# Split weight tiles begin 64, 256, 400 and 464 bytes behind a multiple of 512, and a scan mask is kept in bf16

## The chip, the cores and the metric

The kernel runs on one core of one Trainium2 chip. The metric is the device time of one execution in microseconds, the median of several runs. A run is also profiled once; its rows are in microseconds from the start of the profiled span unless marked ns.

## The reference

One decoder layer for 1024 tokens of width 1024, in float32. After a norm, one wide projection feeds two mixers: RWKV-7 time mixing (8 heads of 64, a recurrent state for each) and attention over at most 256 keys that an indexer selects for each query. Their outputs are merged through sigmoid gates, and a SwiGLU network with 2816 hidden channels follows.

```python
u = rmsnorm(h, norm1_g)
proj = u @ w_in                       # 1024 x 5960
p_rwkv, p_att, p_idx, p_gate = jnp.split(proj, c, axis=-1)
y_a = rwkv7_mix(token_shift(p_rwkv, tshift_mu), ...)
y_b = dsa_attention(q, k, v, q_idx, k_idx, w_idx)
g_a, g_b = jnp.split(jax.nn.sigmoid(p_gate), 2, axis=-1)
merged = g_a * (y_a @ w_o_rwkv) + g_b * (y_b @ w_o_att)
h = h + merged @ w_out
z = rmsnorm(h, norm2_g) @ w_ffn_in
z_gate, z_up = jnp.split(z, 2, axis=-1)
h = h + (jax.nn.silu(z_gate) * z_up) @ w_ffn_out
return rmsnorm(h, normf_g)
```

## The kernel before

The 1024 tokens are two halves of 512. Every large product has activations with channels on the partitions as the moving operand, 128 channels by 512 tokens at a time, and a 128x128 block of weights as the stationary one; a result tile of 128 output channels by 512 tokens gathers in PSUM over eight blocks of input channels (six in the last group of the SwiGLU network).

To keep float32 accuracy in the faster fp32r format, each operand is split into a high part and the rest: hi = x rounded to fp32r, lo = x - hi. `mm3` (L133 to L144) then issues three matmuls for each block: hi weights by hi activations (L138) and by lo activations (L139), in turn block by block, and afterwards lo weights by hi activations (L143). Each matmul is preceded by a load of its own 128x128 weights.

Weights come tile by tile through `weights` (L122 to L129). A DMA brings 128 partitions x 8 blocks x 128 float32, 4096 bytes a partition, into a tile `wst` (three buffers). `split` (L111) makes `whi` on ScalarE (L112) and `wlo` on VectorE (L113, which reads `wst` and `whi`); each has two buffers. All of these tiles begin at a multiple of 512 bytes in their partition, and so does each 512-byte block in them; activations that stream through the matmuls begin at multiples of 512 as well. 231 weight tiles pass through in one execution.

TensorE's order is written out by hand: the program's generators yield after a few matmuls each, and `pump` lets projections, the merge and the SwiGLU network run as fill between the steps of the indexer, RWKV and attention, which are chains of short matmuls with VectorE and ScalarE between. The other engines' orders come from the scheduler, and the splits of weights have a high priority there. Small temporaries `tmp` come in turn from a ring of four buffers of 128x512 float32.

RWKV works on quarters of 256 tokens. Its decay is a running sum in chunks of 64 tokens: `tensor_tensor_scan` (L535) multiplies the sum by a mask, `rmask`, which is 0 at the first token of a chunk and 1 elsewhere, and adds the next value. There are four scans of 128x256 in each quarter, 16 in all. `rwkv_consts` fetches the mask once (L477, on SyncE's queue) at about 348 us, and the tile is float32, 1024 bytes a partition.

Of the kernel before, what the change touches and what calls it, by code (L numbers as in the profile page):

```python
# [11 lines left out]
F32 = mybir.dt.float32  # L12
F32R = mybir.dt.float32r
BF16 = mybir.dt.bfloat16
# [35 lines left out]
def block_kernel(ctx: ExitStack, tc: tile.TileContext, ins: dict, outT: bass.AP, stop=None, dbg=None):  # L50
    nc = tc.nc
    V, A, G, T, SY = nc.vector, nc.scalar, nc.gpsimd, nc.tensor, nc.sync

    cp = ctx.enter_context(tc.tile_pool(name="cp", bufs=1))
    wp = ctx.enter_context(tc.tile_pool(name="wp", bufs=2))
# [52 lines left out]
    def tmp():  # L108
        return tp.tile([128, HT], F32, tag="tmp", name="tmp")

    def split(hi, lo, x):  # L111
        A.activation(hi, x, AF.Copy)  # L112
        V.tensor_tensor(lo, x, hi.bitcast(F32), op=ALU.subtract)  # L113
# [3 lines left out]
    def raw_weights(src, nk=8):  # L117
        st = wp.tile([128, nk, 128], F32, tag="wst", name="wst", bufs=3)
        wq[0].dma_start(st, src)
        return st  # L120

    def weights(src, nk=8, rush=True, st=None):  # L122
        with tc.high_priority() if rush else nullcontext():
            if st is None:
                st = raw_weights(src, nk)
            hi = wp.tile([128, nk, 128], F32R, tag="whi", name="whi")
            lo = wp.tile([128, nk, 128], F32R, tag="wlo", name="wlo")
            split(hi, lo, st)
        return hi, lo  # L129

# [134 lines left out]
    def proj(ct, us, out, off=0):  # L265
        w = weights(ins["w_in"][ct])
        for half, u in enumerate(us):
            ps = acc()
            o = off if half == 0 else 0
            yield from mm3(ps[:, :HT - o], w, u, tok=slice(o, HT))  # L270
            out(half, ps)
# [45 lines left out]
    def proj_rope(ct, us, pj, cs, dst, scale=1.0, off=0):  # L317

        wa, wb = weights(ins["w_in"][ct]), weights(ins["w_in"][ct + 1])
        for half, u in enumerate(us):  # L320
            o = off if half == 0 else 0
            ps = acc()
            yield from mm3(ps[:, :HT - o], wa, u, tok=slice(o, HT))
            ab = rope_a(cs, ps, half, o, scale)
            ps = acc()
            yield from mm3(ps[:, :HT - o], wb, u, tok=slice(o, HT))
            rope_b(cs, ps, ab, pj, dst(half), half, o, scale)
# [12 lines left out]
    def first(us, xp, pj, cp2, cs):  # L340
# [6 lines left out]
        load_x(1, hs[1], range(8))  # L347
        SY.dma_start(cs, ins["rope"])
        ws = [weights(None, st=st, rush=False) for st in (st0, st1)]
        sqs, raws = [], []  # L350
        for half, h in enumerate(hs):
# [117 lines left out]
    def rwkv_consts(p):  # L469
        blk = p.tile([128, 128], F32, name="blk")  # L470
        SY.dma_start(blk, ins["consts"][:, K_BO, :])
        wup = p.tile([128, 512], F32, name="wup")
        SY.dma_start(wup, ins["wa_up"])
        gup = p.tile([128, 512], F32, name="gup")
        SY.dma_start(gup, ins["g_up"])
        rmask = p.tile([128, 256], F32, name="rmask")
        SY.dma_start(rmask, ins["rmask"])  # L477
        ind8 = p.tile([8, 512], F32R, name="ind8")
        t = tmp()
        SY.dma_start(t[0:8, :], ins["ind8"])  # L480
        A.activation(ind8, t[0:8, :], AF.Copy)
        for tag, n in [("wa", 256), ("gd", 256), ("x0", 1024), ("x7", 1024), ("v", 1024), ("x1", 1024), ("x2", 1024),
                       ("x4", 1024), ("x5", 1024), ("x3", 1024), ("AR", 2048), ("rhs", 512), ("UV0", 1024),
                       ("UV1", 1024), ("BK0", 1024), ("BK1", 1024), ("x6", 1024)]:
            p.tile([128, n], F32, tag=tag, name=tag)
        cmask = p.tile([128, 192], F32, name="cmask")
        SY.dma_start(cmask, ins["cmask"])
        p.tile([128, 64], F32, name="edge")
        ind2 = smp.tile([128, 2], F32, name="ind2")
        SY.dma_start(ind2, ins["ind2"])  # L490

        return blk, cmask, wup, gup, rmask, ind2, ind8
# [764 lines left out]
    wq[0] = A  # L1257
    sr, rp = opened("right", "rw")
    consts = rwkv_consts(rp)
    at0 = []  # L1260

# [127 lines left out]
```

## Time and profile before

| | |
|---|---|
| median of 3 runs | 1791.27 us (1788.14 to 1796.37) |
| the profiled execution | 1791.53 us, span 1789.7 us |
| granted TensorE clock, mean | 0.987 |
| PE matmul busy | 1735.4 us, 97% |
| PE weight load busy | 1428.1 us, 80% |
| VectorE / ScalarE busy | 1113.0 us / 829.6 us |
| HBM traffic | 135 GB/s over the span |

PE is TensorE's matmuls, PEld its weight loads, which overlap them; DVE is VectorE, ACT ScalarE, POOL GpSimd, SP SyncE, and a q behind an engine's name is its queue. A row of a timeline gives the start, the length, the engine, the line in the kernel, the operation and how many like ones in a row were merged; a bracket behind it tells how long the engine had been idle, and what ended that. A row of a tile's answer gives the number of instructions and their shortest, median and longest time in ns. Matmuls are pipelined, so their shown lengths overlap, and the ends of matmuls are modelled.

### The profile page before, as it was taken

The numbers are of one execution on the slowest core, as the hardware profiler recorded it, in microseconds if no ns is written. First come the engines' busy times: TensorE is split into PE (matmuls) and PEld (weight loads), VectorE is DVE, ScalarE is ACT, GpSimd is POOL, SyncE is SP. The second block draws the span as 40 slices with busy tenths as digits, with TensorE's granted clock in tenths as the row PEclk, the third lists the DMA queues.
The fourth block names the chain that finished last, engine by engine and source line by source line (L and its number), as shares of the span: only waits on it lengthen the run. The fifth ranks groups of instructions, "written<-read, shape, count | busy, mean of one in ns | idle before, by whom it ended". The sixth has DMA issues, their size and how long they took to land.

```text
span 1789.7 us, 26478 instructions
## 1 busy us (share of the span) xinstructions
PE 1735.4 (97%) x10112; PEld 1428.1 (80%) x10112; DVE 1113.0 (62%) x2113; ACT 829.6 (46%) x1527; POOL 94.4 (5%) x116
## 2 busy tenths in 40 slices
PE   7999999999999899999999999999999999999997
PEld 6888888788887677777788788888788888888875
DVE  6779899866568358958865455434575564454454
ACT  6355998543455886345333355522334332232232
POOL 0000000010020010001001211000000000000000
PEclk9999999999999899999999999999999999999998
DMA  5542224536275434643243944143555344434432
GB/s 205 164 137 94 97 98 142 169 88 178 90 210 150 119 113 146 215 123 104 78 118 118 261 122 124 60 149 120 183 186 166 114 142 145 138 96 148 143 100 103
DMA packets 129838, 243.97 MB, mean 136 GB/s; under 512 B 36408, under 2 KB 57528, under 8 KB 129584
## 3 DMA queue, kind: packets, MB, share of 16 engines
q1 hardware_dynamic: 106752, 169.95, 30.7%
q10 hardware_dynamic: 15120, 46.18, 8.3%
q0 software_dynamic: 7840, 26.15, 5.4%
q8 instruction: 80, 1.31, 0.3%
q14 instruction: 46, 0.38, 0.1%
HBM read 189.29 MB, written 52.95 MB: 135 GB/s over the span
## 4 chain that ended last, share of the span: by engine, by line
PE 74%; DVE 11%; ACT 6%; issue 5%; DMA 3%; POOL 0%; DVEq 0%; POOLq 0%; ACTq 0%
PE acc L138 20%; PE acc L139 19%; PE acc L143 19%; PE mix L1016 2%; PE mix L992 2%; PE mix L1006 2%; DVE wlo L113 2%; ACT junk L907 2%; ACT junkl L907 2%; PE mix L859 1%; DMA wst<-in_w_ffn_in 1%; DVE junk L904 1%; PE mix L764 1%; PE mix L752 1%; PE mix L638 1%
## 5 line engine op out<-in xcount | busy, mean ns | idle before, releaser
L113 DVE TENSOR_TENSOR wlo<-wst,whi 128x1024 fp32r<-128x1024 f32 (+1 forms) x231 | 278.2, 1204 | 356.9 <-PE acc L143 165.7
L112 ACT ACTIVATE whi<-wst 128x1024 fp32r<-128x1024 f32 (+1 forms) x231 | 241.0, 1044 | 315.7 <-PE acc L139 266.6
L138 PE MATMUL acc<-zhi,whi 128*128 128x512 f32 x672 | 266.7, 397 | 2.0 <-DVE tmp L1164 2.0
L139 PE MATMUL acc<-zlo,whi 128*128 128x512 f32 x672 | 262.8, 391 | 0.0
L143 PE MATMUL acc<-zhi,wlo 128*128 128x512 f32 x672 | 171.6, 393 | 0.0
L138 PEld LDWEIGHTS acc<-zhi,whi 128*128 128x128 f32 x672 | 126.6, 188 | 29.1 <-DVE tmp L1164 2.4
L139 PEld LDWEIGHTS acc<-zlo,whi 128*128 128x128 f32 x672 | 126.8, 189 | 24.6
L143 PEld LDWEIGHTS acc<-zhi,wlo 128*128 128x128 f32 x672 | 124.4, 188 | 25.6 <-issue 1.0
L138 PE MATMUL acc<-u1hi,whi 128*128 128x512 f32 x352 | 141.4, 402 | 0.0
L138 PE MATMUL acc<-fhi,whi 128*128 128x512 f32 x352 | 138.6, 394 | 2.5 <-ACT fhi L112 2.5
L138 PE MATMUL acc<-u0hi,whi 128*128 128x512 f32 (+1 forms) x352 | 135.7, 388 | 4.2 <-DVE tmp L280 2.4
L139 PE MATMUL acc<-flo,whi 128*128 128x512 f32 x352 | 137.8, 392 | 0.9 <-DVE flo L113 0.9
L139 PE MATMUL acc<-u1lo,whi 128*128 128x512 f32 x352 | 138.6, 394 | 0.0
L139 PE MATMUL acc<-u0lo,whi 128*128 128x512 f32 (+1 forms) x352 | 134.1, 383 | 0.0
L143 PE MATMUL acc<-u1hi,wlo 128*128 128x512 f32 x352 | 90.7, 398 | 0.0
L143 PE MATMUL acc<-fhi,wlo 128*128 128x512 f32 x352 | 89.0, 393 | 0.0
L143 PE MATMUL acc<-u0hi,wlo 128*128 128x512 f32 (+1 forms) x352 | 86.8, 387 | 0.0
L112 ACT ACTIVATE fhi<-tmp 128x512 fp32r<-128x512 f32 x44 | 27.8, 631 | 120.0 <-DVE tmp L1168 119.9
L138 PEld LDWEIGHTS acc<-fhi,whi 128*128 128x128 f32 x352 | 66.4, 189 | 18.3 <-ACT fhi L112 4.2
L138 PEld LDWEIGHTS acc<-u0hi,whi 128*128 128x128 f32 x352 | 66.3, 188 | 17.5 <-issue 2.6
L139 PEld LDWEIGHTS acc<-flo,whi 128*128 128x128 f32 x352 | 66.4, 189 | 15.7 <-DVE flo L113 2.2
L138 PEld LDWEIGHTS acc<-u1hi,whi 128*128 128x128 f32 x352 | 66.9, 190 | 14.3 <-issue 0.9
(302 smaller groups left out, 3143.7 us busy)
## 6 DMA issues: line engine op xcount, KB each, us to landing
wst<-in_w_ffn_in SPq DMA_DIRECT2D x72, 512.0 KB, 3.6
wst<-in_w_in ACTq DMA_DIRECT2D x36, 512.0 KB, 3.7
wst<-in_w_fo SPq DMA_DIRECT2D x28, 512.0 KB, 3.6
wst<-in_w_in SPq DMA_DIRECT2D x27, 512.0 KB, 3.6
k<-d_k POOLq DMA_DIRECT2D x24, 512.0 KB, 9.0
h<-in_xT SPq DMA_DIRECT2D x32, 256.0 KB, 5.2
d_g<-tmp ACTq DMA_DIRECT2D x32, 256.0 KB, 3.0
tmp<-d_g SPq DMA_DIRECT2D x32, 256.0 KB, 3.1
```

The lines of the kernel that those rows point to most:

```text
L112: A.activation(hi, x, AF.Copy)
L113: V.tensor_tensor(lo, x, hi.bitcast(F32), op=ALU.subtract)
L138: T.matmul(ps, whi[:, wk + k, :], ahi[:, ak + k, tok], start=k == 0, stop=False)
L139: T.matmul(ps, whi[:, wk + k, :], alo[:, ak + k, tok], start=False, stop=False)
L143: T.matmul(ps, wlo[:, wk + k, :], ahi[:, ak + k, tok], start=False, stop=k == nk - 1)
L638: T.matmul(pss[g][:, hh * 128:(hh + 1) * 128], BK[ct // 2][ro, ct % 2, pr, 2 * pa:2 * pa + 2, :].rearrange("p s t -> p (s t)"), AR[ro, ct, ...
L752: T.matmul(as_[h % 2][:, ct * 64:ct * 64 + 64], AR[ro, ct, c, :, :].rearrange("p s t -> p (s t)"), st[ro, ct, :], start=True, stop=True)
L764: T.matmul(ps[ba:ba + 64, hc], TT[ba:ba + 64, pr, h, :], rhs[ba:ba + 64, hc], start=True, stop=True)
L907: A.activation(junka[:, :n], y, AF.Sign, bias=z[:, i:i + 1], accum_out=cnt[:, i:i + 1])
L992: T.matmul(ps[:, :w], q[bi // 2][:, e, bi % 2 * 128:bi % 2 * 128 + 128], k[:, i, e, c:c + w], start=i == 0, stop=i == 1)
L1006: T.transpose(ps[:, j * 128:(j + 1) * 128], L[:, (c + j) * 128:(c + j + 1) * 128], ident)
L1016: T.matmul(py[64 * e:64 * e + 64, bi * 128:(bi + 1) * 128], v[:, j, 64 * e:64 * e + 64], pts[e][j // 4][:, j % 4, :], start=j == b, stop=j ...
```

## The change

`whi` and `wlo` are allocated as tiles of 1024 + 48 and 1024 + 16 float32 a partition, and the 1024 that are used begin 16 and 4 float32 behind the tile's start. With two buffers of each, one behind the other, the used parts begin 64 and 256 bytes (whi) and 400 and 464 bytes (wlo) behind a multiple of 512. A six-block tile takes the first 768 of the 1024. This needs 512 bytes a partition more.

The mask becomes bf16, which needs 512 bytes less: its values arrive as float32 in a `tmp` tile, and VectorE copies them into the bf16 tile. All other tiles that move do so by exactly 512 bytes. TensorE's instructions and their order are the same as before; VectorE has one more, the copy.

```diff
+    def place(tag, off, more, nk):
+        w = wp.tile([128, 1024 + more], F32R, tag=tag, name=tag)
+        return w[:, off:off + nk * 128].rearrange("p (k c) -> p k c", k=nk)
+
     def weights(src, nk=8, rush=True, st=None):
         with tc.high_priority() if rush else nullcontext():
             if st is None:
                 st = raw_weights(src, nk)
-            hi = wp.tile([128, nk, 128], F32R, tag="whi", name="whi")
-            lo = wp.tile([128, nk, 128], F32R, tag="wlo", name="wlo")
+            hi, lo = place("whi", 16, 48, nk), place("wlo", 4, 16, nk)
             split(hi, lo, st)
         return hi, lo
...
-        rmask = p.tile([128, 256], F32, name="rmask")
-        SY.dma_start(rmask, ins["rmask"])
+        rmask = p.tile([128, 256], BF16, name="rmask")
+        t = tmp()
+        SY.dma_start(t[:, 0:256], ins["rmask"])
+        V.tensor_copy(rmask, t[:, 0:256])
         ind8 = p.tile([8, 512], F32R, name="ind8")
```

## The prediction

> **What bounds the kernel now.** I read the page's busy shares and its chain of waits first, then the rows of the tile wlo, then the timeline at places where matmuls of known width stand in a row.
>
> ```profile
> span 1789.7 us, 26478 instructions
> PE 1735.4 (97%) x10112; PEld 1428.1 (80%) x10112; DVE 1113.0 (62%) x2113; ACT 829.6 (46%) x1527; POOL 94.4 (5%) x116
> PE 74%; DVE 11%; ACT 6%; issue 5%; DMA 3%; POOL 0%; DVEq 0%; POOLq 0%; ACTq 0%
> PE acc L138 20%; PE acc L139 19%; PE acc L143 19%; PE mix L1016 2%; PE mix L992 2%; PE mix L1006 2%; DVE wlo L113 2%; ACT junk L907 2%; ACT junkl L907 2%; PE mix L859 1%; DMA wst<-in_w_ffn_in 1%; DVE junk L904 1%; PE mix L764 1%; PE mix L752 1%; PE mix L638 1%
> ```
>
> TensorE sets the time: 74% of the chain is PE, and 58% are the three lines whose weights come out of the tiles that move: L138 and L139 read whi, L143 reads wlo. So the question is whether a place of these tiles changes the pace of those matmuls. A weight load is a separate instruction on PEld that runs beside the matmul before it.
>
> How many there are comes from the rows of the tile wlo:
>
> ```profile
> L143 PEld LDWEIGHTS acc<-zhi,wlo x672: 186/188/192, 848.1 to 1739.0; 128*128 128x128 f32 x168
> L143 PE MATMUL acc<-zhi,wlo x672: 387/389/504, 848.3 to 1739.2; 128*128 128x512 f32 x168
> L143 PE MATMUL acc<-u0hi,wlo x352: 279/389/504, 45.2 to 510.5; 128*128 128x512 f32 x164, 128*128 128x256 f32 x12
> L143 PE MATMUL acc<-u1hi,wlo x352: 387/389/632, 50.7 to 693.4; 128*128 128x512 f32 x176
> L143 PE MATMUL acc<-fhi,wlo x352: 388/389/628, 953.3 to 1773.5; 128*128 128x512 f32 x176
> L143 PE MATMUL acc<-yhi,wlo x128: 387/389/397, 707.3 to 1337.7; 128*128 128x512 f32 x128
> L143 PE MATMUL acc<-mhi,wlo x128: 387/389/793, 756.3 to 1383.5; 128*128 128x512 f32 x128
> ```
>
> The first row is the loads (188 ns each as shown). The counts of the matmuls, ahead of the colon, make 1984; 12 of the 176 sampled u0 rows are 256 wide, so about 24 of its 352 are. That leaves about 1960 wlo matmuls of 512 columns, and by the code twice as many with whi: 5880 in all.
>
> Their pace, and that of narrower ones (start, length of the merged stretch, count at the end):
>
> ```profile
> 1562.53 1.98 PE L143 MATMUL acc<-zhi,wlo 128*128 128x512 f32 x8
> 35.90 1.12 PE L143 MATMUL mix<-u0hi,wlo 128*128 128x256 f32 x8
> 1419.13 1.05 PE L240 MATMUL mix<-kc,rs 128*128 128x128 f32 x8
> L240 PE MATMUL mix<-kc,rs x32: 271/275/581, 843.7 to 1780.2; 128*128 128x128 f32 x32
> ```
>
> A matmul is shown as 0.389 us long, but they are pipelined; start to start is (1.98 - 0.389) / 7 = 0.2273 us at 512 columns. At 256 columns, whose shortest row is 279 ns, it is (1.12 - 0.28) / 7 = 0.120 us. At 128 columns, each with a load of its own, it is (1.05 - 0.275) / 7 = 0.111 us. So 256 columns more cost 0.1073 us, 512 columns cost 0.2146, and 0.0127 us of each matmul does not scale with its width. And a load of 128 columns together with its short matmul needs no more than 0.111 us, less than half of the 0.227 that the wide matmul beside it gives. 5880 x 0.2273 = 1337 us of the 1790 go at this pace.
>
> **The change part by part.** *The places.* All weight tiles begin at a multiple of 512 bytes now; afterwards the two whi buffers begin 64 and 256 behind one, the two wlo buffers 400 and 464. Number, size, order and buffering of loads, splits and matmuls stay. Three accesses see the new places: PE's weight loads, ACT's write of whi, and DVE's read of whi and write of wlo.
>
> Weight loads first. If they took time from the matmul that streams beside them, a matmul with no load beside it would end earlier. The trace has that case, in the last two output tiles of the kernel:
>
> ```profile
> 1768.25 1.52 PE L143 MATMUL acc<-fhi,wlo 128*128 128x512 f32 x6
> 1769.61 0.39 PE L138 MATMUL acc<-fhi,whi 128*128 128x512 f32 x1
> 1769.81 0.69 DVE L1188 TENSOR_TENSOR h<-h,acc 128x512 f32<-128x512 f32 x1 [1.08 <-PE acc L143]
> 1772.33 1.52 PE L143 MATMUL acc<-fhi,wlo 128*128 128x512 f32 x6
> 1773.89 0.69 DVE L1188 TENSOR_TENSOR h<-h,acc 128x512 f32<-128x512 f32 x1 [2.00 <-PE acc L143]
> 1776.07 0.97 PEld L227 LDWEIGHTS mix<-kc,sacc 128*128 128x128 f32 x8 [2.65 <-DVE sacc L221]
> ```
>
> The ends that the profile gives for matmuls are modelled, so I take the waiting VectorE as the clock. In the first group the sixth matmul starts at 1768.25 + 1.52 - 0.389 = 1769.38, the next matmul (whose weights must be loaded meanwhile) follows at 1769.61, and L1188 starts at 1769.81: 0.43 us after. In the second group the sixth starts at 1773.46, no load comes until 1776.07, and L1188 starts at 1773.89: again 0.43. Rounding to 0.01 us hardly leaves room for 0.0127 us, so at today's places the load takes nothing from the matmul beside it.
>
> Now a load from another place. No row shows a 128-column block that starts off a multiple of 512. From below its price is nothing; from above it may grow from at most 0.111 us to 0.227, about double, before the matmul beside it stops covering it. I take nothing, because the nearest rows, the loads of today, show no meeting with the stream and more than half of the cover unused. [...]
>
> ACT and DVE:
>
> ```profile
> L112 ACT ACTIVATE whi<-wst x231: 831/1061/1067, 4.7 to 1764.4; 128x1024 fp32r<-128x1024 f32 x108, 128x768 fp32r<-128x768 f32 x8
> L113 DVE TENSOR_TENSOR wlo<-wst,whi x231: 951/1224/1227, 7.9 to 1765.8; 128x1024 fp32r<-128x1024 f32 x108, 128x768 fp32r<-128x768 f32 x8
> ACT whi L112 <- PE acc L139: 266.6, 164, 5.3
> ```
>
> One pair of tiles is split in 1.06 + 1.22 = 2.3 us and feeds 24 matmuls of 0.227 = 5.4 us, and ACT stands waiting 266.6 us in all for PE to give a whi buffer back. A few ns more or less on a split are hidden by that wait; were the cover gone, 10 ns on each of 231 pairs would be 2.3 us.
>
> *The mask.* A 128x256 DMA goes into a tmp tile, DVE copies it to bf16, and the 16 scans read the copy. The rows of that time:
>
> ```profile
> 347.26 0.29 DVE L532 TENSOR_SCALAR gd<-gd 128x256 f32<-128x256 f32 x1
> 347.79 0.68 SPq L477 DMA_DIRECT2D rmask<-in_rmask  x1
> 350.28 1.23 DVE L113 TENSOR_TENSOR wlo<-wst,whi 128x1024 fp32r<-128x1024 f32 x1 [2.73 <-ACT whi L112]
> 353.54 2.13 PE L143 MATMUL acc<-u0hi,wlo 128*128 128x512 f32 x8
> 354.43 0.77 DVE L551 TENSOR_SCALAR x<-x,hb 128x256 f32<-128x256 f32 x2 [2.92 <-ACT x L528]
> DMA to landing us min/median/max: 4.2/4.2/4.2
> L535 DVE TENSOR_TENSOR_SCAN x<-rmask,x x16: 662/666/685, 356.4 to 841.5; 128x256 f32<-128x256 f32 x16
> ```
>
> In the order of the changed program the copy stands on DVE right behind L532 and ahead of that wlo split. Issued at 347.79 and landing 4.2 later, the mask is there at 352.0; the copy, priced by L532 on the same 128x256, ends at 352.3. So the split, queued behind the wait, moves from 350.28 to 352.3 and ends at 353.5 instead of 351.5; PE's L143 on it begins at 353.54. The wait of 2 us is just covered: I count 0.1 us for it, and up to 1 if the transfer is later. The next on DVE, L551, waits for ACT until 354.43 anyway. The transfer keeps its place and size in SP's queue. The tile taken from the ring of four tmp tiles shifts which buffer each later tmp gets, not how many there are; around here ACT gets a wait on the copy before it may reuse that buffer, two raw tiles later (356), past the copy's end. The scans: VectorE reads one operand narrower; from 0 to, if a scan were halved, -16 x 0.33 = -5 us, at most partly on the chain; I take 0, as the other operand and the result stay f32 and 666 ns for 256 elements is no matter of bytes.
>
> **Sum.** The profiled execution took 1791.53 us with a span of 1789.7, beside a median of 1791.27 (1788.14 to 1796.37). 1791.53 + 0 + 0 + 0.1 = 1791.6; put on the median, 1791.4. I say 1791.5, with 1788 to 1796 as this case's own range. What a measurement of this kernel can tell from no change is about 0.5%, 9 us, so "same" reaches from 1782 to 1800.
>
> **Rivals.** *Faster:* the fixed 0.0127 us of each matmul comes from operands that all begin at the same place behind a multiple of 512, the streamed ones and the weights, and spreading the places takes it away. For it: that part is there at 512 and at 256 columns alike, as a cost per load would be. Against it: the 0.43 and 0.43 above. If only wlo gains (64 and 256 are still multiples of 64, 400 and 464 are not), 1960 x 0.0127 = 25 us: 1766. If all gain, 5880 x 0.0127 = 75 us: 1717. [...]
>
> *Slower:* the pace of 0.2273 is one that a run of equal matmuls settles into. After short matmuls it is uneven at first:
>
> ```profile
> 1414.78 0.40 PE L1136 MATMUL acc<-zhi,wlo 128*128 128x512 f32 x1
> 1415.01 0.40 PE L1136 MATMUL acc<-zhi,whi 128*128 128x512 f32 x1
> 1415.24 0.40 PE L1136 MATMUL acc<-zhi,wlo 128*128 128x512 f32 x1
> 1415.48 3.81 PE L1140 MATMUL acc<-zlo,whi 128*128 128x512 f32 x16
> ```
>
> Three steps here take 1415.48 - 1414.78 = 0.70, 0.233 each; the 16 after them take (3.81 - 0.39) / 15 = 0.228. If loads from odd places end late enough to keep PE unsettled, 0.006 us are lost per matmul: 1960 x 0.006 = 12 us with wlo alone (1803), 5880 x 0.006 = 35 us with all (1827). It decides as soon as the steady pace leaves 0.227, and a load that passes twice its 0.111 us would do it by itself. Against it: the wide cover.
>
> *That it does nothing but the mask* is the forecast; a mask that lands 2 us later would add 2 us and stay within "same".
>
> **How the numbers follow.** Forecast 0.50. Faster, wlo alone 0.16 and all 0.10: 0.26. Slower, wlo alone 0.15 and all 0.09: 0.24. The unlikely wide ones (0.10 and 0.09) are left out of the range, which therefore runs from 1764 to 1808, past 1766 and 1803 by the few us of the mask and the spread.
>
> **What would show it.** Right: runs of eight L143 matmuls still take 1.98 us, eight at 256 columns 1.12, whi and wlo splits 1.06 and 1.22, and DVE's copy of the mask ends near 352.3 with L143 behind it not waiting. Wrong: a steady start-to-start other than 0.227 on L143 alone (the places of wlo), or on L138 and L139 too (those of whi), or weight loads whose median leaves 188 ns.

## The result: 1.2% slower

After: 1814.43 us (median of 4 runs, 1810.98 to 1816.18) beside 1793.51 us before (4 runs, 1788.14 to 1796.37); ratio 1.0118, 95% interval 1.0087 to 1.0149. That is 20.9 us more, and above the predicted range of 1764 to 1808. The profiled execution took 1815.27 us, at a granted clock of 0.987 as before.

The page of the kernel after, the lines for the span and the engines:

```profile
span 1813.4 us, 26480 instructions
PE 1759.6 (97%) x10112; PEld 1430.4 (79%) x10112; DVE 1114.3 (61%) x2114; ACT 830.5 (46%) x1527; POOL 94.4 (5%) x116
```

L138, L139 and L143 are now L142, L143 and L147. The span grew by 23.7 us, and PE's busy time by 24.2 (from 1735.4) over the same 10112 matmuls. DVE and ACT differ by about 1 us. So the time went into the matmuls themselves and not into waits; the starts below confirm it.

The rows of tile wlo show it as a median:

```profile
L147 PEld LDWEIGHTS acc<-zhi,wlo x672: 186/188/192, 857.4 to 1762.0; 128*128 128x128 f32 x168
L147 PE MATMUL acc<-zhi,wlo x672: 387/394/505, 857.7 to 1762.3; 128*128 128x512 f32 x168
```

The row of tile whi:

```profile
L142 PE MATMUL acc<-zhi,whi x672: 387/393/505, 853.9 to 1760.2; 128*128 128x512 f32 x168
```

The load is still 188 ns and the medians of the splits are the same within 1 ns (1060 for whi, 1224 for wlo); the wide matmul's median went from 389 to 394 and 393 ns. A wide matmul in a steady row is shown about 162 ns longer than its start-to-start time (389 beside 227), so 394 means some 232.

From the timeline before, the eight wlo matmuls ahead of those that the prediction shows at 1562.53; then the timeline of the kernel after, over two weight tiles:

```profile
1557.09 1.98 PE L143 MATMUL acc<-zhi,wlo 128*128 128x512 f32 x8
```

```profile
1565.62 2.02 PE L147 MATMUL acc<-zhi,wlo 128*128 128x512 f32 x8
1567.48 0.39 PE L142 MATMUL acc<-zhi,whi 128*128 128x512 f32 x1
...
1571.21 2.03 PE L147 MATMUL acc<-zhi,wlo 128*128 128x512 f32 x8
1573.07 0.40 PE L142 MATMUL acc<-zhi,whi 128*128 128x512 f32 x1
...
1576.71 1.55 PE L147 MATMUL acc<-zhi,wlo 128*128 128x512 f32 x6
```

The first column is all that is needed. In the kernel after, the eight wlo matmuls take 1567.48 - 1565.62 = 1.86 us, 0.2325 each, in both tiles. The sixteen whi matmuls behind them take 3.73 us in the first tile (0.2331 each, whi at 64) and 3.64 in the second (0.2275, whi at 256). Together the 24 matmuls of a tile take 5.59 and 5.50 us; before, they took 1562.53 - 1557.09 = 5.44. With 5880 / 24 = 245 such groups, 245 x 0.105 = 26 us would follow if every group stood in so steady a row; 20.9 were measured.

Over all starts in the trace, with each step put down to the weights whose load runs beside it and steps over 241 ns left out, the mean is 227.5 ns for whi and 227.4 for wlo before; after, it is 232.9 beside loads from 64, 228.6 from 256, 233.1 from 400 and 231.7 from 464. What these steps take over 226.67 ns sums to 4.4 us before and 26.6 after: +22 us of the 23.7 by which the span of the profiled execution grew. About 13 of the 22 us lie beside loads of whi and 9 beside loads of wlo.

### The profile page after: what moved, and what is told of

It reads as the page before. It is cut to its first block, busy times and chain, and to the rows that moved or that the text cites. A ratio compares the mean times of both kernels' runs of the same rounds, so it can differ in the third digit from the quotient of the medians.

```text
span 1813.4 us, 26480 instructions
## 1 busy us (share of the span) xinstructions
PE 1759.6 (97%) x10112; PEld 1430.4 (79%) x10112; DVE 1114.3 (61%) x2114; ACT 830.5 (46%) x1527; POOL 94.4 (5%) x116
## 4 chain that ended last, share of the span: by engine, by line
PE 86%; DVE 5%; issue 3%; DMA 3%; ACT 2%; POOL 0%; POOLq 0%; SPq 0%; DVEq 0%; ACTq 0%
PE acc L147 23%; PE acc L142 23%; PE acc L143 23%; PE mix L1022 2%; PE mix L998 2%; PE mix L1012 2%; PE mix L865 2%; DMA d_h<-tmp 1%; PE mix L770 1%; DVE wlo L113 1%; PE mix L758 1%; DMA wst<-in_w_ffn_in 1%; PE mix L644 1%; DMA tmp<-d_yb 1%; PE mix L780 1%
## 5 line engine op out<-in xcount | busy, mean ns | idle before, releaser
L142 PE MATMUL acc<-zhi,whi 128*128 128x512 f32 x672 | 267.1, 397 | 4.2 <-ACT whi L112 2.3
L143 PE MATMUL acc<-zlo,whi 128*128 128x512 f32 x672 | 264.5, 394 | 0.0
L147 PE MATMUL acc<-zhi,wlo 128*128 128x512 f32 x672 | 174.6, 397 | 0.0
L142 PEld LDWEIGHTS acc<-zhi,whi 128*128 128x128 f32 x672 | 126.3, 188 | 33.1 <-ACT whi L112 2.7
L143 PEld LDWEIGHTS acc<-zlo,whi 128*128 128x128 f32 x672 | 126.3, 188 | 26.9
L147 PEld LDWEIGHTS acc<-zhi,wlo 128*128 128x128 f32 x672 | 124.4, 188 | 28.3 <-issue 1.0
L142 PE MATMUL acc<-u1hi,whi 128*128 128x512 f32 x352 | 141.8, 403 | 0.0
L142 PE MATMUL acc<-fhi,whi 128*128 128x512 f32 x352 | 139.2, 395 | 2.5 <-ACT fhi L112 2.5
L143 PE MATMUL acc<-flo,whi 128*128 128x512 f32 x352 | 139.1, 395 | 0.9 <-DVE flo L113 0.9
L143 PE MATMUL acc<-u1lo,whi 128*128 128x512 f32 x352 | 139.3, 396 | 0.0
L142 PE MATMUL acc<-u0hi,whi 128*128 128x512 f32 (+1 forms) x352 | 136.7, 390 | 2.5 <-DVE tmp L284 2.5
L143 PE MATMUL acc<-u0lo,whi 128*128 128x512 f32 (+1 forms) x352 | 135.8, 388 | 0.0
L147 PE MATMUL acc<-u1hi,wlo 128*128 128x512 f32 x352 | 92.5, 403 | 0.0
L147 PE MATMUL acc<-fhi,wlo 128*128 128x512 f32 x352 | 91.2, 399 | 0.0
L147 PE MATMUL acc<-u0hi,wlo 128*128 128x512 f32 (+1 forms) x352 | 88.2, 391 | 0.0
L142 PEld LDWEIGHTS acc<-fhi,whi 128*128 128x128 f32 x352 | 66.3, 188 | 19.3 <-ACT fhi L112 4.2
L143 PEld LDWEIGHTS acc<-flo,whi 128*128 128x128 f32 x352 | 66.2, 188 | 17.2 <-DVE flo L113 2.2
L142 PEld LDWEIGHTS acc<-u0hi,whi 128*128 128x128 f32 x352 | 66.7, 190 | 16.3 <-issue 2.6
L147 PEld LDWEIGHTS acc<-fhi,wlo 128*128 128x128 f32 x352 | 66.7, 190 | 15.6
```

The costliest lines, as they stand in the source:

```text
L142: T.matmul(ps, whi[:, wk + k, :], ahi[:, ak + k, tok], start=k == 0, stop=False)
L143: T.matmul(ps, whi[:, wk + k, :], alo[:, ak + k, tok], start=False, stop=False)
L147: T.matmul(ps, wlo[:, wk + k, :], ahi[:, ak + k, tok], start=False, stop=k == nk - 1)
```

## The experiments

Unless a text says otherwise, "at 64" means 64 bytes behind a multiple of 512, and the streamed operands stay at multiples of 512. The distance of a matmul is the place of its weights less the place of its stream, counted modulo 256. Each kernel of streams was executed once, with a granted clock of 0.998 to 1.0. Letters for theories hold within one quoted text. The kernels with rows of their own line numbers have wlo's matmuls at L147 or L149.

**The place alone, in steady rows.** A kernel of its own: 64 matmuls in a row, two weight blocks in turn, no other work.

```python
for i in range(64):
    T.matmul(ps, w[:, i % 2 * 128:i % 2 * 128 + 128],
             move[:, i // 2 % 2 * 512:i // 2 % 2 * 512 + 512], start=i == 0, stop=i == 63)
```

> A kernel of its own that leaves the layer out: streams of 64 fp32r matmuls of 512 columns, all weights of a stream from one tile that begins a given number of bytes behind a multiple of 512 (0 to 496 in steps of 16, and 4, 8, 12, 20, 260); the name of the tile tells the number. First with the streamed operand at a multiple of 512, then 64 and then 16 bytes behind one, at last with 128 columns, where the load is the longer part. Theory A (the place of the load alone sets the pace): with the stream at 0, 0 and 256 give 0.227 us a matmul, 64 gives 0.233, 400 about 0.233 and 464 about 0.232, and moving the stream changes nothing. Theory B (what counts is the distance from stream to load): with the stream at 64 the good places move to 64 and 320, and 0 gets 0.233. Theory C (a steady place never costs, only the change from one place to another does): 0.227 everywhere once a stream runs. If the load itself became longer, the streams of 128 columns would leave 0.111 us at the slow places.

Its timeline; mov0b is the stream at 0, at64b the weights at 64. The pace is (length - 0.39) / 63:

```profile
127.22 15.09 PE L53 MATMUL ps<-mov0b,at64b 128*128 128x512 f32 x64
290.85 14.69 PE L53 MATMUL ps<-mov0b,at240b 128*128 128x512 f32 x64
305.38 14.68 PE L53 MATMUL ps<-mov0b,at256b 128*128 128x512 f32 x64
454.18 15.10 PE L53 MATMUL ps<-mov0b,at400b 128*128 128x512 f32 x64
513.43 15.00 PE L53 MATMUL ps<-mov0b,at464b 128*128 128x512 f32 x64
557.72 14.84 PE L60 MATMUL ps<-mov64b,at0b 128*128 128x512 f32 x64
676.12 14.69 PE L60 MATMUL ps<-mov64b,at64b 128*128 128x512 f32 x64
1681.12 7.31 PE L74 MATMUL ps<-mov0b,at16b 128*128 128x128 f32 x64
1709.71 7.31 PE L74 MATMUL ps<-mov0b,at64b 128*128 128x128 f32 x64
```

256 and 240 keep 14.68 to 14.69 (0.2268 us; 226.67 ns by the last 40 starts), 64 and 400 take 15.09 to 15.10 (0.2333), 464 takes 15.00 (0.2319). With the stream itself at 64, weights at 64 are the fast ones and weights at 0 are not. For streams at 0 every place r from 0 to 240 agrees with r + 256. Streams at 64 repeat the figures of streams at 0 at the same distances, but for distances 16 and 240, which took 226.7 in some rows and 228.3 to 233.3 in others. Streams at 16 do not: weights at 16 took 233.3 ns there, at 0 231.7, and at 48, 112 and 208 226.7. No row of 512 columns goes below 226.65 ns. The last two rows are 128 columns wide. By the prediction's 0.0127 us a matmul and 0.1073 us for 256 columns, a stream of that width would ask for 0.066 us (an estimate), so the author took the load for the longer part there. The rows take 7.31 at either place, 0.112 us a matmul (0.111 in the prediction): nothing in them is longer for weights at 64.

**The mask alone.** The change's second half, with the weight tiles as before.

> Only the bf16 mask; all weight tiles back at multiples of 512. Theory A and B: no change, 0 to +1 us, matmuls again 0.227 us start to start. Rival (the wait on the mask's transfer, the copy and the tmp ring cost the time): all of the +21 us, with L143's pace unchanged.

1796.83 us (10 runs) beside 1794.82; ratio 1.0008, interval 0.9996 to 1.0020. The mask is not the cause.

**whi's places alone, and wlo's alone**, both with the mask:

```diff
-            hi, lo = place("whi", 16, 48, nk), place("wlo", 4, 16, nk)
+            lo, hi = place("wlo", 0, 0, nk), place("whi", 16, 48, nk)   # whi at 64 and 256, wlo at 0; streams at 384 or 0
```

> The mask in bf16, wlo at multiples of 512, only whi at 64 and 256 behind one. Theory A: of the matmuls' extra time in the changed kernel, summed by the tile whose load runs beside them, about +13 us belong to whi, nearly all to the buffer at 64; so +13 us. Theory C (the changes between places cost): about as much as the full change, since each weight tile still changes place: +18 to +21 us. Rival (only wlo, off a multiple of 64, costs): 0.

```diff
-            hi, lo = place("whi", 16, 48, nk), place("wlo", 4, 16, nk)
+            hi = place("whi", 0, 0, nk)
+            wp.tile([128, 96], F32, tag="gap", name="gap", bufs=1)
+            lo = place("wlo", 4, 16, nk)                                # whi at 0, wlo at 400 and 464
```

> The mask in bf16, whi at multiples of 512, only wlo at 400 and 464 behind one. Theory A: about +9 us, all on the matmuls with wlo and the first few with whi after them. Rival (only wlo, off a multiple of 64, costs): all of the +21 us.

wlo alone: 1802.19 us beside 1794.82, ratio 1.0037 (1.0025 to 1.0048), 7 us. In its trace the steps beside loads from 464 average 231.6 ns, but those beside loads from 400 only 227.8, though 233.1 in the kernel after. There the whi tile ahead was at 64, here it is at 0: a tile's pace also hangs on what ran before it.

The run called whi alone took 1811.28 us, ratio 1.0078 (1.0052 to 1.0103), which is 14 us by the ratio and 16 by the medians. It does not isolate whi. Its layout is 2 x 48 x 4 = 384 bytes longer than the weights at multiples of 512, where the whole change is 384 + 128 = 512 longer and wlo alone fills up to 512 with a gap. So what lies behind the weights in the same half of the memory moved by 384 too, and 4128 of the 6096 wide matmuls streamed from there, 128 behind a multiple of 256. From its timeline, two starts of wlo with streams at 384, then two of the second half, whose streams stayed at multiples of 512:

```profile
1234.91 2.02 PE L147 MATMUL acc<-zhi,wlo 128*128 128x512 f32 x8
1240.45 2.03 PE L147 MATMUL acc<-zhi,wlo 128*128 128x512 f32 x8
1566.87 1.98 PE L147 MATMUL acc<-zhi,wlo 128*128 128x512 f32 x8
1572.42 2.00 PE L147 MATMUL acc<-zhi,wlo 128*128 128x512 f32 x8
```

The eight wlo matmuls, whose weights are at 0 throughout, span 2.02 to 2.03 us in the first pair and 1.98 to 2.00 in the second. Split by the stream's place, the steps of this run fit a rule of distance rather than one of the weights' place alone. With streams at 384, loads from wlo at 0 and whi at 256 (distance 128) average 232.5 and 232.6 ns, and loads from whi at 64 (distance 192) 229.9. With streams at multiples of 512, loads from whi at 64 average 233.0 and from whi at 256 226.9; loads from wlo at 0 average 227.0 behind whi at 256 and 230.8 behind whi at 64, again by what ran before. What whi's places cost by themselves was not measured; the 13 us of the steps in the kernel after are the nearest figure.

**Place or distance, and the width.** The same kind of kernel, with streams at 0, 32, 128, 192 and 240 and weights at chosen distances from each, then narrower matmuls.

> A kernel of its own as before, the layer left out. The streamed operand 0, 32, 128, 192 and 240 bytes behind a multiple of 256, for each the weights at a chosen distance from it (0, 64, 128, 192, 240, 16, 32, 96, 160, counted up to 256); then 384 and 256 columns with the stream at 0 and weights at 0, 64, 128, 192, 240 and 16. Theory B (distance from stream to load, counted modulo 256): distance 0 gives 0.227 us with every stream, 64 and 128 give 0.233, and nothing is under 0.227. Theory A (place of the load alone): with every stream it is the weights at 0 and 240 that give 0.227. By width: if the extra time is paid once for each load, 256 and 384 columns lose the same 6 to 7 ns as 512 at 64 and 128; if it is a share of the stream's time they lose half and three quarters of that.

```profile
141.87 14.67 PE L52 MATMUL ps<-mov32b,at32b 128*128 128x512 f32 x64
156.39 15.09 PE L52 MATMUL ps<-mov32b,at96b 128*128 128x512 f32 x64
540.48 15.09 PE L52 MATMUL ps<-mov240b,at240b 128*128 128x512 f32 x64
683.92 11.47 PE L52 MATMUL ps<-mov0b,at64b 128*128 128x384 f32 x64
717.58 11.26 PE L52 MATMUL ps<-mov0b,at240b 128*128 128x384 f32 x64
739.78 7.83 PE L52 MATMUL ps<-mov0b,at0b 128*128 128x256 f32 x64
747.45 7.70 PE L52 MATMUL ps<-mov0b,at64b 128*128 128x256 f32 x64
```

For streams at 0, 32, 128 and 192 the figures follow the distance and not the place: 0, 16 and 240 give 226.7 ns, 192 gives 229.0, 128 gives 232.4, 32, 64 and 160 give 233.3, 96 gives 234.3. Each stream met the distances in the same order, though, and what ran before can matter: weights at 16 under streams at 0, free here, had taken 233.3 ns in the first sweep, behind an unsettled row (one slower than the 226.7 of a calm row), and weights at 128 233.3 instead of 232.4. Streams at 240 broke the rule as those at 16 had: distance 0 was slow there (third row), distances 32, 96 and 192 were free. So the rule is shown for streams at 0, 32, 64, 128 and 192, and not for those two. At 384 columns the distance 64 costs (11.47 - 11.26) / 63 = 3.3 ns instead of 6.7; at 256 columns it gains 2 ns. So the price is neither a fixed one per load nor one per column.

**All four buffers at 64, and all at 256**, with the mask:

```diff
-            hi, lo = place("whi", 16, 48, nk), place("wlo", 4, 16, nk)
+            wp.tile([128, 16], F32, tag="gap", name="gap", bufs=1)      # 64 instead of 16: all at 256
+            hi, lo = place("whi", 0, 0, nk), place("wlo", 0, 0, nk)
+            wp.tile([128, 112], F32, tag="rest", name="rest", bufs=1)   # 64 instead of 112: all at 256
```

> The mask in bf16; all four weight tiles 64 bytes behind a multiple of 512, every other tile at the place that it has in the changed kernel (activations that stream at multiples of 512). Both theories: every one of some 6190 wide matmuls settles at 0.233 instead of 0.227, so +38 to +41 us. Theory C (only changes between places cost): 0, since no tile changes place.

> The same with all four weight tiles 256 bytes behind a multiple of 512. Theories A and B: no change against the kernel before, 0.227 everywhere. Rival (anything but a multiple of 512 costs): +20 us or more.

At 64: 1825.04 us beside 1795.03, ratio 1.0162 (1.0142 to 1.0182), 30 us. At 256: 1792.90, ratio 0.9992 (0.9975 to 1.0010). The 30 us are less than the 38 to 41 expected; the steps of that trace, summed as above, are 33 us over those before. At 256 nothing is lost: a tile that leaves its multiple of 512 by 256 bytes is free. All at 64 has also the case on which the prediction rested, the last two output tiles. Its timeline:

```profile
1798.95 1.56 PE L149 MATMUL acc<-fhi,wlo 128*128 128x512 f32 x6
1800.35 0.39 PE L144 MATMUL acc<-fhi,whi 128*128 128x512 f32 x1
1800.55 0.69 DVE L1196 TENSOR_TENSOR h<-h,acc 128x512 f32<-128x512 f32 x1 [1.20 <-PE acc L149]
...
1803.15 1.56 PE L149 MATMUL acc<-fhi,wlo 128*128 128x512 f32 x6
1804.75 0.69 DVE L1196 TENSOR_TENSOR h<-h,acc 128x512 f32<-128x512 f32 x1 [2.12 <-PE acc L149]
```

By the prediction's own arithmetic the sixth matmul starts at 1798.95 + 1.56 - 0.39 = 1800.12, and VectorE 0.43 later; in the second group at 1804.32, and VectorE again 0.43 later. Yet the six start (1800.35 - 1798.95) / 6 = 0.2333 apart. In the kernel with the largest loss the test gives the same 0.43 and 0.43 as before: it cannot see this cost.

**Both shifted by 64.** A 64-byte gap at the head of the pool moves the weights and everything behind them in the same half of the memory: the first half's activations move along, the second half's stay (1968 of 6096 wide matmuls then stream at another place than their weights).

```diff
+    wp.tile([128, 16], F32, tag="gap", name="gap", bufs=1)
```

> Like the kernel with all weight tiles at 64, but what lies behind them in the same stack moves by 64 bytes too: the projections' inputs and the first half's activations stream from 64 behind a multiple of 512 (4128 wide matmuls), the second half's from multiples of 512 (1968). Theory B: only the second half's lose 6.7 ns each, +13 us. Theory A: all lose, +38 to +41 us.

1806.38 us, ratio 1.0061 (1.0044 to 1.0079), 11 us with the same weights at 64 that cost 30 above. The rows of wlo and of its timeline:

```profile
L149 PE MATMUL acc<-u0hi,wlo x352: 279/389/504, 45.3 to 508.9; 128*128 128x512 f32 x164, 128*128 128x256 f32 x12
L149 PE MATMUL acc<-zhi,wlo x672: 387/393/504, 847.1 to 1751.7; 128*128 128x512 f32 x168
1553.19 2.03 PE L149 MATMUL acc<-zhi,wlo 128*128 128x512 f32 x8
1558.80 2.03 PE L149 MATMUL acc<-zhi,wlo 128*128 128x512 f32 x8
```

u0, which moved with the weights, has its 389 again; in the second half, whose z stayed, a tile takes 5.61 us. The same weights at the same places have both paces in one execution. It is the place of the weights against that of the stream. By the steps, those with streams at 64 average 227.8 ns and those with streams at 0 233.3.

**One odd matmul in 24.** A kernel of its own: all at 0 but for one matmul (L57) with weights at 256, 64 or 128, or with its stream at 64; L56 is the one ahead of it, L58 the one behind. At the end, places reached from a calm or an unsettled stretch.

> A kernel of its own, the layer left out. Streams with weights and streamed operand at multiples of 512, in which one matmul in 24 is odd: its weights 256, then 64, then 128 behind, at last its streamed operand 64 behind. The one before the odd one is L56, the odd one L57, the next L58 and L59. A settled matmul of 0.227 us is shown 389 ns long, and a longer step shows as a longer matmul. If the load's reads meet the reads of the matmul that streams beside it, the odd load at 64 or 128 first lengthens L56 (the load of L57's weights runs beside it), and the odd stream first lengthens L57. If a matmul pays for the place of its own weights, it is L57 that is first lengthened in both, and L56 keeps 389. At 256 nothing is lengthened. Then streams of 64 at 16, 144 and 208, each reached once from 0 and once from 64: if the pace depends on the place alone, both ways give the same; if it also depends on where the stream comes from, they differ by up to 6.7 ns.

The rows of the lines L56 and L57, first with the odd weights at 64, then with them at 128:

```profile
L56 PE MATMUL ps<-mov0b,at0b x15: 388/388/388, 106.2 to 182.7; 128*128 128x512 f32 x15
L57 PE MATMUL ps<-mov0b,at64b x15: 397/397/398, 106.5 to 182.9; 128*128 128x512 f32 x15
L56 PE MATMUL ps<-mov0b,at0b x15: 396/396/396, 193.6 to 269.9; 128*128 128x512 f32 x15
L57 PE MATMUL ps<-mov0b,at128b x15: 397/397/397, 193.8 to 270.2; 128*128 128x512 f32 x15
```

At 256 the odd one changes nothing (389 throughout). At 128 the matmul ahead, beside which the odd weights load, is longer by 7 ns; at 64 it is not, and the odd one itself is the first that is. With the odd stream at 64 (weights at 0), L57 is shown 398 ns and L58 402. So the runs do not say which two accesses meet. The timeline of three streams at the end:

```profile
373.15 14.67 PE L68 MATMUL ps<-mov0b,at16b 128*128 128x512 f32 x64
387.65 15.10 PE L68 MATMUL ps<-mov0b,at64b 128*128 128x512 f32 x64
402.59 15.09 PE L68 MATMUL ps<-mov0b,at16b 128*128 128x512 f32 x64
```

They show two paces at one place: weights at 16 take 14.67 behind a calm stretch and 15.09 behind one at 64. Weights at 144 do the same; those at 208 take 15.00 either way.

**Own weights or the next one's.** Places 0 and d in turn: once a matmul's weights and stream share a place and the next weights, which load beside it, are d away; once its stream lies where the next weights lie, and its own weights are d away.

```python
T.matmul(*one(ps, at, at, i), ...)                                    # own: at = d if i % 2 else 0
T.matmul(*one(ps, 0 if i % 2 else d, d if i % 2 else 0, i), ...)      # following: stream, weights
```

> A kernel of its own: 64-matmul streams of 512 columns with two places, 0 and d bytes behind a multiple of 512, used in turn (d = 64, 128, 192, 32), each after a calm stream with all at 0. In 'own' a matmul's weights and its stream share a place, so that the load running beside it (the next one's weights) is d or 256 - d away. In 'following' a matmul's stream has the place of the next one's weights, so that the load beside it is at distance 0 and its own weights are d away. Theory A, the load that runs beside a stream meets it: 'following' keeps the calm 0.2267 us from start to start, 'own' takes a mean between the paces of distances d and 256 - d, some 0.231 for 64 and 192, 0.2324 for 128, 0.231 for 32. Theory B, a matmul's own weights decide: the two change sides, 'own' 0.2267 and 'following' 0.231 to 0.2324. Theory C, any change of place from matmul to matmul unsettles the pace: both above 0.228.

The calm streams around them in the timeline (64 matmuls of "own" at d = 64 lie between the first two, of "following" between the next two, and of "own" at d = 128 between the last two):

```profile
6.78 16.24 PE L55 MATMUL ps<-mov0b,at0b 128*128 128x512 f32 x64 [6.78 <-ACT mov0b L30]
37.67 14.68 PE L55 MATMUL ps<-mov0b,at0b 128*128 128x512 f32 x64
67.02 14.71 PE L55 MATMUL ps<-mov0b,at0b 128*128 128x512 f32 x64
96.19 14.71 PE L55 MATMUL ps<-mov0b,at0b 128*128 128x512 f32 x64
```

A calm stream ends its steps 0.39 - 0.23 = 0.16 us ahead of its shown end. "Own" therefore took 37.67 - (6.78 + 16.24 - 0.16) = 14.81 us, 0.2314 each, and "following" 67.02 - (37.67 + 14.68 - 0.16) = 14.83, 0.2317 each; "own" at 128 took 14.62, 0.2284 each. By the starts the last 40 of both average 231.7 ns at d = 64; at 128 it is 228.4 and 229.9, at 192 231.7 and 231.7, at 32 231.7 and 230.0. Neither "the load beside" nor "a matmul's own weights" alone keeps the calm pace. What unsettles is that either differs, or that places change from matmul to matmul; these runs leave that open.

**Does the distance rule hold in the whole kernel?** Two layouts it prices differently: whi at 16 and 240 with wlo at 0, and all four at 192.

```diff
+            hi = place("whi", 4, 56, nk)                                # whi at 16 and 240
+            wp.tile([128, 16], F32, tag="gap", name="gap", bufs=1)
+            lo = place("wlo", 0, 0, nk)
```

> The whole kernel with the bf16 mask; the whi buffers begin 16 and 240 bytes behind a multiple of 512, the wlo buffers at one; streams at multiples of 512. Theory A, the distance between a load and the stream beside it decides: in the streams measured alone 16, 240 and 0 bytes all gave 0.2267 us, so nothing is lost, 1795 give or take 5 beside a kernel before of 1795. Theory C, any change of place from tile to tile unsettles the pace, as with two places used in turn (0.2284 to 0.232) and as wlo at 0 was slow behind whi at 64 and 256: 6 to 14 us slower, 1801 to 1809. A rule of whole multiples of 64, 128 or 256 bytes, by which 16 and 240 are worse than 64: at least as slow as all weights at 64, 1825.

The second is the kernel with all at 256, with gaps of 48 and 80 in place of 64 and 64.

> The whole kernel with the bf16 mask and all four weight buffers 192 bytes behind a multiple of 512, streams at multiples of 512. Theory A: streams alone at distance 192 take 0.2290 us from start to start, 0.0023 over the calm pace; 5880 x 0.0023 = 13.5 us, and with the share that the kernel with all weights at 64 showed of its sum (30 of 39 us) 10: 1802 to 1809. If only being off the place counts, and not how far: as with all weights at 64, 1825.

The timelines, first of the near places, then of all at 192:

```profile
1557.93 1.98 PE L149 MATMUL acc<-zhi,wlo 128*128 128x512 f32 x8
1563.37 1.98 PE L149 MATMUL acc<-zhi,wlo 128*128 128x512 f32 x8
```

```profile
1562.72 2.00 PE L149 MATMUL acc<-zhi,wlo 128*128 128x512 f32 x8
1568.22 2.00 PE L149 MATMUL acc<-zhi,wlo 128*128 128x512 f32 x8
```

Near places: 5.44 us a tile, 1796.63 us beside 1794.61, ratio 1.0011 (0.9999 to 1.0022). Three different places that are all within 16 bytes of the streams' (modulo 256) cost next to nothing, so a change of place from tile to tile does no harm by itself, and the rule is none of multiples: 16 is free, 64 is not. (The text's point on wlo at 0 being slow behind whi rests in the main on the streams that had moved by 384 in the run called whi alone.) All at 192: 5.50 us a tile, 1802.05 us, ratio 1.0042 (1.0025 to 1.0059), 7 us where the rule's 13.5, scaled by what all at 64 had kept of its sum, gave 10; inside the range that was given.

No layout that was run beats the kernel before (all at 256, at 0.9992, cannot be told from it): its steps beside loads of whi and wlo already average 227.5 and 227.4 ns, and no stream of 512 columns settled below 226.65 at any place or distance tried.

## Why the prediction was wrong, point by point

**The step that failed** is the price of the place, set to nothing because "at today's places the load takes nothing from the matmul beside it", read from VectorE starting 0.43 us after a matmul with a load beside it and 0.43 after one without. Two faults lie in it. The test measures from a matmul's start to the start of the engine that waits for its end; the cost shows only from start to start, and all at 64 gives 0.43 and 0.43 with a pace of 0.2333. And a reading at distance 0 was carried over to places for which no row existed, although both ends of the range there had been left open. In its place stands a term of up to 6.67 ns for each wide matmul: 245 tile groups x 0.105 us = 26 us by the steady stretch, 20.9 in the whole. That it hangs on the weights' place against the stream's is shown by the kernel with both shifted, in which matmuls with the same weights take 227.8 ns beside streams at 64 and 233.3 beside streams at 0; which two accesses meet stays open.

**The cover** (a load may double its 0.111 us before it shows) was the author's estimate, and no run put it to the test: the load was not seen to get longer (188 ns in the kernel, 7.31 us for 64 narrow matmuls at 16 and at 64), and still the wide matmul beside it lost time.

**The slower rival** came near in size and had the mechanism wrong. It gave +12 us for wlo alone and +35 for all; wlo alone measured +7, and all at 64 +30. Its 0.006 us came from the unsettled starts of a row, and 0.2333 against 0.2267 is what the places give; no run shows that the two have one cause, so the nearness is luck as far as is known. Its cause, loads that end late, does not fit the narrow rows, which take 7.31 us at 64 as at 16, nor the shifted kernel, in which matmuls beside the same loads have both paces (227.8 and 233.3 ns). And it had only two cases, wlo alone or all; the change was a third, with whi's second buffer at the harmless 256: between the two at 1814, and above the range, from which the case of all was left out.

**The faster rival** (the 0.0127 us goes when places are spread) is refuted: no place in the sweeps settles below 226.65 ns at 512 columns.

**Splits** were right: 1060 and 1224 ns, 1061 and 1224 before. **The mask** was right as well. Its timeline in the kernel after:

```profile
348.78 0.29 DVE L538 TENSOR_SCALAR gd<-gd 128x256 f32<-128x256 f32 x1
353.61 0.29 DVE L483 CAST rmask<-tmp 128x256 bf16<-128x256 f32 x1 [4.54 <-DMA tmp<-in_rmask]
353.82 1.22 DVE L113 TENSOR_TENSOR wlo<-wst,whi 128x1024 fp32r<-128x1024 f32 x1
356.33 2.13 PE L147 MATMUL acc<-u0hi,wlo 128*128 128x512 f32 x8
```

The kernel is 1.52 us behind by then (L538 at 348.78 instead of 347.26), so the copy's end at 353.90 answers to 352.38, where 352.3 was predicted. The split ends at 355.04 and PE starts on it at 356.33: the wait stayed covered, with 1.3 us to spare, as PE itself was 2.8 us behind by then. With the mask alone PE was not behind: its L143 starts at 353.24, 1.93 us after the first of the sixteen matmuls ahead of it, as before, so nothing waited there either. The 16 scans kept their length (667 ns there, 666 before). The mask alone measured 1.0008.

**What would show it** named the right sign: a start-to-start other than 0.227 on L143, L138 and L139. Its other sign, a load median off 188 ns, would have said that nothing had happened: it stayed at 188.

## What to carry to other kernels

Begin the 512-column operand that streams at multiples of 512 bytes and the 128x128 weight blocks at multiples of 256 (226.7 ns a matmul here, 228 to 237 at most other pairs of places), and after any change of a tile's size or of the pool's order look where the tiles behind it went: a run meant to move whi alone moved two thirds of the streams as well. Judge the pace of pipelined matmuls by the starts in a long row: VectorE, which waited for the last one, started 0.43 us after that one's start with steps of 0.2267 us and of 0.2333 alike. A null test for a cost counts only if it has been seen to answer where the cost is present.

## What the runs showed that had not been expected

- fp32r matmuls of 512 columns, each with its own load, settle between 226.67 and 234.3 ns by the distance from stream to weights modulo 256 bytes, for streams at 0, 32, 64, 128 and 192: 0 is free, 16 and 240 are free in most rows and take 228.3 to 233.3 in some, 192 takes 229.0, 128 takes 232.4 to 233.3, 32 and 64 take 233.3, 96 takes 234.3. Streams at 16 and 240 follow another pattern, in which distance 0 took 233.3 and distances 32, 96 and 192 were free.
- The pace has a memory: weights at 16 took 226.7 behind a calm stretch and 233.3 behind one at 64; weights at 144 likewise. In the whole kernel, wlo at 400 took 227.8 behind whi at 0 and 233.1 in the kernel after.
- At 256 columns the order turns: 119.8 ns at distance 0, 117.8 at 64.
- A row of 128 columns, each with its own load, takes about 112 ns a matmul at every place tried (7.31 us for 64, in one row 7.26).
